# Float16 pairs for the gate and up products of FFN groups two and three, in a hybrid attention and mLSTM diffusion layer

## The chip, the cores and the metric

The kernel runs on one core of a Trainium2 chip. The metric is the device time of one execution in microseconds (us), the median of three runs. One more execution is taken by the profiler; its busy times, waits and clocks are those quoted here. The engines are called PE (TensorE; its weight loads, which run beside its matmuls, are PEld), DVE (VectorE), ACT (ScalarE), POOL (GpSimd) and SP (SyncE, which issues nearly all transfers).

## What is computed

The reference is one step of a diffusion backbone with one layer. There are 128 context tokens and 1024 latent tokens, 1152 in all; the model width is 1024 and the FFN width 2816. All arithmetic is float32. Cut to what matters here:

```python
def trunk_layer(x, mods, ...):
    sh1, sc1, g1, sh2, sc2, g2 = mods          # from silu(cond) @ w_ada + b_ada
    h = rmsnorm(x, norm1_w) * (1 + sc1) + sh1
    ... = split(h @ w_in, ...)                 # attention q, k, v; mLSTM q, k, v, o, gates
    attn_o = attention(aq, keys, vals)         # 8 query heads of 64, 2 kv heads, rope
    hm, st_f, st_b = mlstm_bidir(...)          # 4 heads of 128, forward and backward
    x = x + g1 * (concatenate([attn_o, hm]) @ w_out)
    h2 = rmsnorm(x, norm2_w) * (1 + sc2) + sh2
    x = x + g2 * swiglu(h2, w_gu, w_down)
    return x, ...

def swiglu(h, w_gu, w_down):
    g, u = split(h @ w_gu, 2, axis=-1)
    return (silu(g) * u) @ w_down
```

The outputs are the final RMS norm of x for both kinds of token, new keys and values of the context, and the mLSTM states.

## The kernel before

**Stages.** The 1152 tokens are nine blocks of 128, and three blocks make a chunk of 384 tokens. The kernel goes through: load, first norm and modulation (about 0 to 60 us); keys, values, gates and the attention's query projection (60 to 165); four mLSTM heads, with the attention of chunk 0 woven between (165 to 520); the prefill, which is the output projection and second norm of chunk 0 (520 to 617); then the FFN of chunks 0, 1 and 2 (617 to 938, 938 to 1284, 1284 to 1572), the attention of the next chunk being woven beside the first two. The change calls the FFN of these three chunks groups one, two and three.

**Products of nearly float32 precision.** A float32 operand is split into a high part and a rest (hi and lo), and a product is three matmuls: hi·hi, hi·lo, lo·hi. In the FFN both parts are of type fp32r, of four bytes. In the projections of the first stages they are float16 pairs, which needs the operands scaled by a power of two so that they lie in float16's range: class `Scaled` takes the largest absolute value of a weight, by ACT passes with an accumulated sum (an upper bound of the maximum), and `power_scale` (L166–177) turns a bound per partition into a power of two on all partitions. `power_scale` is a small chain over engines: PE transposes the column (L116), DVE reduces it to one number (L171) and makes a power of two and its inverse from its bits in four steps (`powers`, L161–164), PE broadcasts them by a matmul with a row of ones (L175, operands `pv` and `one`), and DVE copies the result (L176).

**An FFN chunk.** `gate_up` (L1319–1341) goes through 22 tiles f of 128 FFN columns, in groups of 4 or 5. For each f it loads a gate piece and an up piece of w_gu (128 partitions x 1024, 512 KB) with `load_piece` (L140–154): SP's transfer into `raw` (two buffers), ACT's cast to the high part `whi` (L152, five buffers), DVE's subtraction for the low part `wlo` (L137, five buffers). Then `products` (L1313–1317) runs 24 matmuls of 128x384 for the piece: eight k, three products each, on the features h2 of the chunk (`aTh`, `aTl`: transposed, 8 x 128 x 384). The activation is tanh on ACT (L1333), two products on DVE (L1334, L1335), a cast on ACT (L1338) and a subtraction on POOL. `down` (L1343–1355) multiplies by w_down in the same fp32r form, 128x512, from pieces loaded in the same way.

**The features.** `norm2` (L1282–1311) makes h2 of a block: ACT scales the row by its inverse norm (`y`, L1294), PE transposes (L116), DVE applies scale2 and shift2 (`fl`, L1304; for chunk 0 also ACT, L1302), ACT casts to `aTh` (L1309), and DVE (POOL in chunk 0) subtracts for `aTl`. norm2 of the next chunk is woven into the `down` of the last group of f (12 to 16 and 17 to 21 are the last two groups; L1479–1481). scale2 and shift2 are computed long before, by the generator `ada`, which finishes just ahead of `kwork` near the end of the query projection (L979–980).

**What sets the order.** Every engine runs its own queue in order. `weave` and `emit` set in which order instructions are written out; a planner with its own costs and priorities (`hot(n)`) then fixes the order on every engine from that. A tile that is reallocated under the same tag waits for the last user of its buffer. Around 162 to 172 us, PE runs four transposes of `qr` (the attention's queries) and then the 72 query matmuls of the first mLSTM head (`q_group`, L808–810); DVE runs the steps of a small inverse square root (L131–133), the copy of `QT` (L654), a 128x1024 subtraction for a float16 pair (`ipair`, L137), subtractions for `qT` and rotary products (L679).

Of the kernel before, what the change touches and what calls it, by code (L numbers as in the profile page):

```python
# [8 lines left out]
F32 = mybir.dt.float32  # L9
F32R = mybir.dt.float32r  # L10
F16 = mybir.dt.float16
BF16 = mybir.dt.bfloat16
# [7 lines left out]
P = 128  # L20
# [25 lines left out]
def hybrid_step(ctx: ExitStack, tc: tile.TileContext, I: dict, O: dict):  # L46
# [11 lines left out]
    def nm(s):  # L58
        uid[0] += 1
        return f"{s}_{uid[0]}"  # L60
# [10 lines left out]
    def emit(gen):  # L71
        for _ in gen:
            pass
# [62 lines left out]
    def sub(out, full, hi, eng):  # L136
        (dve if eng == "dve" else pool).tensor_tensor(out=out, in0=full, in1=hi, op=ALU.subtract)  # L137

    def load_piece(srcs, shape, raw=None, own=None):

        a, b = shape
        n = a * b

        def view(t):
            return t[:, :n].rearrange("p (a b) -> p a b", b=b)

        raw = raw or wp.tile([P, 1024], F32, name=nm("raw"), tag="raw", bufs=2)
        hi = own[0] if own else wp.tile([P, 1024], F32R, name=nm("whi"), tag="whi", bufs=5)
        lo = own[1] if own else wp.tile([P, 1024], F32R, name=nm("wlo"), tag="wlo", bufs=5)
        for part, ap_ in srcs:  # L150
            dma(part(view(raw)), ap_)
        nc.scalar.copy(hi[:, :n], raw[:, :n])  # L152
        sub(lo[:, :n], raw[:, :n], hi[:, :n].bitcast(F32), "dve")
        return view(hi), view(lo)
# [78 lines left out]
    bcol = cp.tile([P, 48], F32, name="bcol")  # L233
    ncol = cp.tile([P, 16], F32, name="ncol")
    vsc = cp.tile([P, 4], F32, name="vsc")

    es_a = ExitStack()
    pA = es_a.enter_context(tc.tile_pool(name="pA", bufs=4, space=PSUM, reuse_waits="tile"))
# [738 lines left out]
    emit(steps)  # L977
    groups_in[1].made = groups_in[1].pairs()
    emit(ada)  # L979
    emit(kwork)  # L980
    es_r.close()
    es_h.close()
# [94 lines left out]
    def a_tiles():  # L1077
        return (hp.tile([P, KD, CT], F32R, name=nm("aTh"), tag="b2"),
                hp.tile([P, KD, CT], F32R, name=nm("aTl"), tag="b3"))

    def new_x1(c):
        x1 = hp.tile([P, CB, D], F32, name=nm("x1"), tag=f"b{4 + c % 2}")
# [199 lines left out]
    def norm2(c, a, i):  # L1282

        x1 = a["x1"][i]
        if "h2" not in a:
            a["h2"] = a_tiles()
        th, tl = a["h2"]
        r = a["rs"][i]
        both = ap2.tile([P, KD, P], F32, name=nm("fl"), tag="pr", bufs=2)
        cnd = 0 if c * CB + i == 0 else 1  # L1290
        for half in range(2):
            with hot(800):
                y = fp.tile([P, 512], F32, name=nm("y"), tag="y", bufs=2)
                act(y, x1[:, half * 512 : (half + 1) * 512], AF.Copy, scale=r)  # L1294
                ps = bank()
                for j in range(4):
                    transpose(ps[:, j * P : (j + 1) * P], y[:, j * P : (j + 1) * P])
                full = both[:, half * 4 : half * 4 + 4]
                for j in range(4):
                    k = half * 4 + j  # L1300
                    if j == 0 and c == 0:
                        act(full[:, j, :], ps[:, j * P : (j + 1) * P], AF.Identity, scale=scale2[:, k, cnd : cnd + 1], bias=shift2[:, k, cnd : cnd + 1])  # L1302
                        continue
                    dve.tensor_scalar(  # L1304
                        out=full[:, j, :], in0=ps[:, j * P : (j + 1) * P],
                        scalar1=scale2[:, k, cnd : cnd + 1], scalar2=shift2[:, k, cnd : cnd + 1],
                        op0=ALU.mult, op1=ALU.add)
                oh = th[:, half * 4 : half * 4 + 4, i * P : (i + 1) * P]
                nc.scalar.copy(oh, full)  # L1309
                sub(tl[:, half * 4 : half * 4 + 4, i * P : (i + 1) * P], full, oh.bitcast(F32), "pool" if c == 0 else "dve")  # L1310
            yield True

    def products(ps, wh, wl, th, tl):  # L1313
# [2 lines left out]
            mm(ps, wh[:, k, :], tl[:, k, :], start=False, stop=False)  # L1316
            mm(ps, wl[:, k, :], th[:, k, :], start=False, stop=(k == KD - 1))  # L1317

    def gate_up(a, f0, nf):  # L1319
        th, tl = a["h2"]  # L1320
        acts = a["act"] = []
        for f in range(f0, f0 + nf):
            if True:
                pg, pu = bank(), bank()
                for off, ps in ((0, pg), (D_FF, pu)):
                    src = w_gu[:, off + f * P : off + (f + 1) * P].rearrange("(k p) n -> p k n", p=P)
                    wh, wl = load_piece([(full_view, src)], (KD, P))
                    products(ps[:, 0:CT], wh, wl, th, tl)
                    yield 6
                parts = [(slice(0, CT), pg[:, 0:CT], pu[:, 0:CT])]  # L1330
            tn = fp.tile([P, CT], F32, name=nm("tn"), tag="tn", bufs=2)
            for cs, g, u in parts:
                act(tn[:, cs], g, AF.Tanh, scale=0.5)  # L1333
                dve.scalar_tensor_tensor(out=tn[:, cs], in0=tn[:, cs], scalar=1.0, in1=u, op0=ALU.add, op1=ALU.mult)  # L1334
                dve.tensor_tensor(out=tn[:, cs], in0=tn[:, cs], in1=g, op=ALU.mult)  # L1335
# [98 lines left out]
    for tag, bufs in (("gl", 1), ("gx", 1), ("t2", 3)):  # L1434
        ft.tile([P, 512], F32, name=f"lay_{tag}", tag=tag, bufs=bufs)
    fp = ctx.enter_context(tc.tile_pool(name="fp", bufs=1, side="right", reuse_waits="tile"))

    cur, nxt = {}, {}
    cur["x1"], nxt["x1"] = new_x1(0), new_x1(1)
# [11 lines left out]

    def groups(c, a, lst):
        for f0, nf in lst:
            yield from gate_up(a, f0, nf)
            yield from down(c, a, f0, nf, 0)
            yield from down(c, a, f0, nf, 1)

# [10 lines left out]
    for c in range(NCH):  # L1468
        if c + 1 < NCH:
            main = groups(c, cur, GROUPS[:NG])  # L1470
            for _ in range(4):
                next(main)
            weave(main, chain(previous(c, cur), att), 18 * sum(nf for _, nf in GROUPS[:NG]) - 24, 50)
            emit(att)
            attn_out(nxt, oT, out_gates())
            emit(groups(c, cur, GROUPS[NG:-1]))
            f0, nf = GROUPS[-1]
            emit(gate_up(cur, f0, nf))
            n2 = chain(*[norm2(c + 1, nxt, i) for i in range(CB)])  # L1479
            weave(chain(down(c, cur, f0, nf, 0), down(c, cur, f0, nf, 1)), n2, 6 * nf, 8)  # L1480
            emit(n2)
            if c + 2 < NCH:
                oT = []
                att = attention(c + 2, oT, set())
            nxt["prev"] = cur
            cur = nxt
            nxt = cur["next"] = {}
        else:
            main = groups(c, cur, LAST[:-1])
            for _ in range(4):  # L1490
                next(main)
            weave(main, previous(c, cur), 24, 3)
            emit(main)
            emit(gate_up(cur, *LAST[-1]))
            down_last(c, cur, *LAST[-1])


# [50 lines left out]
```

## Time and profile before

| | |
|---|---|
| median of 3 runs | 1574.08 us (1573.49 to 1574.66) |
| the profiled execution's own time | 1574.08 us |
| its span, first to last instruction | 1572.3 us |
| mean granted clock of PE | 0.979 |
| read from and written to memory | 183.79 MB, 13.26 MB |
| gate/up matmuls 128x384 fp32r (L1315–1317) | 3 x 1056, 353 to 356 us busy each |
| float16 matmuls 128x384 of a head's projection (L484) | 288, 94.1 us busy |
| casts and subtractions of weight pieces | 216 each, 222.3 us of ACT, 260.4 us of DVE (some of another shape among them) |

How to read it: a row of a group has the line, the engine, the operation, the output and its inputs, the shape, the count, then busy time and the mean of one in ns, then the idle time of the engine just before them and what ended it. A timeline row has start and duration in us first, and idle time with its releaser in brackets. Matmuls are pipelined, so a duration overlaps the next start; the rate of a stream is read from its starts. A window's row has the busy time and count of each engine, the granted clock of PE, the mean busy share of the 16 DMA engines, and GB/s.

### The profile page before, as it was taken

What the parts mean: (1) busy time and instruction counts of PE and PEld (TensorE: products, weight loads), DVE (VectorE), ACT (ScalarE), POOL (GpSimd) and SP (SyncE); (2) the same over time, 40 slices, a digit from 0 to 9 for tenths busy, and PEclk for the clock granted to TensorE, in tenths of its full rate; (3) what the DMA queues carried; (4) which work ended last, traced back from release to release, by engine and by line L of the source; (5) the groups of instructions that cost most, each with busy time, mean ns of one, the idle gap of its engine ahead of it and who ended that gap; (6) DMA issues with size and microseconds to landing.
All of it is one profiled execution on the core that took longest, in us unless ns stands there. A gap on an engine that the chain in (4) does not pass through costs nothing.

```text
span 1572.3 us, 23397 instructions
## 1 busy us (share of the span) xinstructions
PE 1487.7 (95%) x8539; PEld 1247.3 (79%) x8539; DVE 1022.9 (65%) x2025; ACT 771.8 (49%) x1409; POOL 271.4 (17%) x357
## 2 busy tenths in 40 slices
PE   6899999999999689999999999999999999999996
PEld 3544567676766468898998989989898989999995
DVE  4878554737659576677555677877866585554555
ACT  4754465847656344545432444556552443323332
POOL 0213333322343242100110101000010101001111
PEclk9899999999999799999999999999999999999998
DMA  9664323523556847767555447878763545544441
GB/s 360 186 182 157 97 68 41 121 47 68 114 150 162 265 80 197 184 174 175 154 154 149 147 126 236 195 170 180 179 162 114 168 133 168 161 130 138 143 139 54
DMA packets 387881, 236.91 MB, mean 151 GB/s; under 512 B 170198, under 2 KB 346790, under 8 KB 387766
## 3 DMA queue, kind: packets, MB, share of 16 engines
q1 hardware_dynamic: 385110, 231.84, 54.1%
q10 hardware_dynamic: 2656, 3.58, 1.1%
q8 instruction: 67, 1.10, 0.3%
q14 instruction: 48, 0.39, 0.1%
HBM read 183.79 MB, written 13.26 MB: 125 GB/s over the span
## 4 chain that ended last, share of the span: by engine, by line
PE 77%; DVE 11%; DMA 5%; ACT 4%; issue 2%; SPq 0%; POOL 0%; ACTq 0%; DVEq 0%; POOLq 0%
PE mm L1316 11%; PE mm L1317 11%; PE mm L1315 11%; PE mm L1115 5%; PE mm L1116 5%; PE mm L1117 5%; PE S L1035 3%; PE wi L483 3%; PE wi L485 3%; PE wi L484 3%; PE mm L116 2%; PE mm L1147 1%; PE mm L1148 1%; PE mm L1149 1%; PE po L1060 1%
## 5 line engine op out<-in xcount | busy, mean ns | idle before, releaser
L152 ACT CAST whi<-raw 128x1024 fp32r<-128x1024 f32 (+1 forms) x216 | 222.3, 1029 | 411.0 <-PE mm L1316 156.5
L137 DVE TENSOR_TENSOR wlo<-raw,whi 128x1024 fp32r<-128x1024 f32 (+1 forms) x216 | 260.4, 1206 | 202.9 <-ACT whi L152 202.3
L1316 PE MATMUL mm<-aTl,whi 128*128 128x384 f32 x1056 | 355.7, 337 | 2.7 <-DVE aTl L137 2.7
L1317 PE MATMUL mm<-aTh,wlo 128*128 128x384 f32 x1056 | 354.3, 336 | 0.0
L1315 PE MATMUL mm<-aTh,whi 128*128 128x384 f32 x1056 | 353.3, 336 | 0.0
L137 POOL TENSOR_TENSOR hl<-tn,hl 128x384 fp32r<-128x384 f32 x66 | 84.4, 1279 | 840.0 <-ACT hl L1338 748.3
L1316 PEld LDWEIGHTS mm<-aTl,whi 128*128 128x128 f32 x1056 | 198.5, 188 | 3.9 <-DVE aTl L137 3.3
L1315 PEld LDWEIGHTS mm<-aTh,whi 128*128 128x128 f32 x1056 | 198.1, 188 | 0.6
L1317 PEld LDWEIGHTS mm<-aTh,wlo 128*128 128x128 f32 x1056 | 198.4, 188 | 0.0
L1116 PE MATMUL mm<-wlo,hl 128*128 128x512 f32 x372 | 145.7, 392 | 0.0
L1115 PE MATMUL mm<-whi,hl 128*128 128x512 f32 x372 | 144.3, 392 | 0.0
L1117 PE MATMUL mm<-whi,hl 128*128 128x512 f32 x372 | 143.4, 392 | 0.0
L483 PE MATMUL wi<-ipair,hT 128*128 128x384 f16 (+2 forms) x408 | 135.6, 335 | 1.7 <-ACT hT L507 1.2
L484 PE MATMUL wi<-ipair,hT 128*128 128x384 f16 (+2 forms) x408 | 135.6, 335 | 0.0
L485 PE MATMUL wi<-ipair,hT 128*128 128x384 f16 (+2 forms) x408 | 132.1, 335 | 1.0 <-DVE hT L137 1.0
L1042 DVE SCALAR_TENSOR_TENSOR pl<-pr,st,ph 128x1152 f16<-128x1152 f32 (+1 forms) x72 | 96.0, 1333 | 31.7 <-ACT ph L1041 31.4
L1037 DVE TENSOR_REDUCE st<-S 128x1 f32<-128x1152 f32 (+1 forms) x72 | 88.9, 1235 | 16.3 <-PE S L1035 16.1
L1038 ACT ACTIVATE pr<-S,st 128x1152 f32<-128x1152 f32 (+1 forms) x72 | 81.3, 1130 | 32.4 <-DVE st L1037 29.3
L1041 ACT ACTIVATE ph<-pr,st 128x1152 f16<-128x1152 f32 (+1 forms) x72 | 83.9, 1165 | 23.8 <-DVE st L1040 6.7
L1035 PE MATMUL S<-kst,qT 128*128 128x384 f32 (+1 forms) x400 | 87.6, 349 | 4.8 <-ACT pr L1038 4.8
L1104 DVE TENSOR_TENSOR t<-mm,gl 128x512 f32<-128x512 f32 x102 | 69.1, 687 | 26.2 <-DMA gl<-g_d 11.5
L1117 PEld LDWEIGHTS mm<-whi,hl 128*128 128x128 f32 x372 | 69.9, 188 | 14.2
(375 smaller groups left out, 2538.4 us busy)
## 6 DMA issues: line engine op xcount, KB each, us to landing
raw<-in_w_gu_dram SPq DMA_DIRECT2D x132, 512.0 KB
raw<-in_w_down_dram SPq DMA_DIRECT2D x60, 512.0 KB
a<-in_w_ada_dram SPq DMA_DIRECT2D x24, 512.0 KB
gl<-g_d SPq DMA_DIRECT2D x36, 256.0 KB
aw<-in_w_ada_dram SPq DMA_DIRECT2D x16, 512.0 KB
iraw<-in_w_in_dram SPq DMA_DIRECT2D x32, 256.0 KB
raw<-in_w_out_dram SPq DMA_DIRECT2D x12, 512.0 KB
x<-in_x_sample_dram SPq DMA_DIRECT2D x11, 512.0 KB
```

Source lines behind the costliest of these rows:

```text
L137: (dve if eng == "dve" else pool).tensor_tensor(out=out, in0=full, in1=hi, op=ALU.subtract)
L152: nc.scalar.copy(hi[:, :n], raw[:, :n])
L483: mm(ps[:, :n], ah, wh[:, k % 2, c0 : c0 + n], start=(k == 0), stop=False)
L484: mm(ps[:, :n], ah, wl[:, k % 2, c0 : c0 + n], start=False, stop=False)
L485: mm(ps[:, :n], al, wh[:, k % 2, c0 : c0 + n], start=False, stop=(k == KD - 1))
L1035: mm(S[:, n, 0:w], qT[:, h, :], kst[kv][:, t, c0 + n * w : c0 + (n + 1) * w], start=(t == 0), stop=(t == 1))
L1115: mm(ps, ah, wh[:, k % 2, :], start=(k == 0), stop=False)
L1116: mm(ps, ah, wl[:, k % 2, :], start=False, stop=False)
L1117: mm(ps, al, wh[:, k % 2, :], start=False, stop=(k == nk - 1))
L1315: mm(ps, wh[:, k, :], th[:, k, :], start=(k == 0), stop=False)
L1316: mm(ps, wh[:, k, :], tl[:, k, :], start=False, stop=False)
L1317: mm(ps, wl[:, k, :], th[:, k, :], start=False, stop=(k == KD - 1))
```

## The change

Five things are changed; the lines are those of the kernel before.

1. For chunks 1 and 2, gate and up use float16 pairs. `gate_piece` takes the place of `load_piece` there: ACT makes hi as a scaled copy, DVE makes lo in one multiply-and-subtract, both in one buffer of 4 KB per partition, from the tag of `whi` for gate and of `wlo` for up. h2 of these chunks is a float16 pair in one buffer of its own: `half_tiles` gives chunk 1 one of the two buffers of `aTh` and `aTl`, and chunk 2 the other.
2. Chunk 0 keeps fp32r, and an added ACT pass for each of its 44 gate and up pieces (Abs of the 128x1024 raw piece, output to a scratch tile in bfloat16) accumulates sums into `gsum`.
3. `bound_h2` is written out between `ada` and `kwork`: the largest |shift2| and |scale2| bound h2 (norm rows are at most the square root of D), `power_scale` makes the power of two, and scale2 and shift2 are multiplied by it in place; tiny steps keep the inverses.
4. `bound_w_gu` is written out after the last `gate_up` of chunk 0: it reduces `gsum`, runs `power_scale` for the weights' scale, and sets the inverses for chunks 1 and 2.
5. The tanh takes its scale, and the second product its factor, from these inverses in every chunk, so that the second product becomes a fused form. The tiles `guc`, `gsum`, `one2` and two unused ones (`lay_cp`, `lay_fp`) bring the pools to multiples of 128 bytes per partition.

PE has 8130 matmul instructions where it had 8126, DVE 24 instructions more, ACT 44 more; POOL has as many as before.

```diff
+    guc = cp.tile([P, 8], F32, name="guc")
+    gsum = cp.tile([P, 2 * NF], F32, name="gsum")
+    one2 = cp.tile([1, P], F32, name="one2")
+    dve.memset(one2, 1.0)
+    cp.tile([P, 8], F32, name="lay_cp")
...
     emit(ada)
+    def inverses_gu(inv):
+        dve.tensor_scalar(out=guc[:, 4:5], in0=inv, scalar1=0.5, scalar2=None, op0=ALU.mult)
+        dve.tensor_tensor(out=guc[:, 5:6], in0=inv, in1=inv, op=ALU.mult)
+    def bound_h2():
+        b2 = gp.tile([P, 2], F32, name="b2")
+        dve.tensor_reduce(out=b2[:, 0:1], in_=shift2, axis=AX.XY, op=ALU.max, apply_absolute_value=True)
+        dve.tensor_reduce(out=b2[:, 1:2], in_=scale2, axis=AX.XY, op=ALU.max, apply_absolute_value=True)
+        dve.scalar_tensor_tensor(out=b2[:, 1:2], in0=b2[:, 1:2], scalar=float(D) ** 0.5, in1=b2[:, 0:1], op0=ALU.mult, op1=ALU.add)
+        emit(power_scale(gp, one1, b2[:, 1:2], guc[:, 0:2]))
+        for t in (scale2, shift2):
+            dve.tensor_scalar(out=t, in0=t, scalar1=guc[:, 0:1], scalar2=None, op0=ALU.mult)
+        inverses_gu(guc[:, 1:2])
+    def bound_w_gu():
+        b2 = fp.tile([P, 2], F32, name="b2w", tag="s1", bufs=3)
+        dve.tensor_reduce(out=b2[:, 0:1], in_=gsum, axis=AX.X, op=ALU.max)
+        emit(power_scale(fp, one2, b2[:, 0:1], guc[:, 2:4]))
+        dve.tensor_tensor(out=guc[:, 6:7], in0=guc[:, 1:2], in1=guc[:, 3:4], op=ALU.mult)
+        inverses_gu(guc[:, 6:7])
+    bound_h2()
     emit(kwork)
...
+    def half_tiles(c):
+        t = hp.tile([P, 2, KD, CT], F16, name=nm("hF"), tag=("b2", "b3")[c % 2])
+        return t[:, 0], t[:, 1]
...
-            a["h2"] = a_tiles()
+            a["h2"] = a_tiles() if c == 0 else half_tiles(c)
...
+    def gate_piece(a, c, i, src):
+        if c == 0:
+            raw = wp.tile([P, 1024], F32, name=nm("raw"), tag="raw", bufs=2)
+            jk = fp.tile([P, 1024], BF16, name="jg") if "jg" not in a else a["jg"]
+            a["jg"] = jk
+            pieces = load_piece([(full_view, src)], (KD, P), raw=raw)
+            act(jk, raw, AF.Abs, accum_out=gsum[:, i : i + 1])
+            return pieces
+        raw = wp.tile([P, 1024], F32, name=nm("raw"), tag="raw", bufs=2)
+        w = wp.tile([P, 2, 1024], F16, name=nm("wf"), tag=("whi", "wlo")[i % 2], bufs=5)
+        dma(raw.rearrange("p (k n) -> p k n", k=KD), src)
+        hi, lo = w[:, 0], w[:, 1]
+        act(hi, raw, AF.Copy, scale=guc[:, 2:3])
+        dve.scalar_tensor_tensor(out=lo, in0=raw, scalar=guc[:, 2:3], in1=hi, op0=ALU.mult, op1=ALU.subtract)
+        return tuple(v.rearrange("p (k n) -> p k n", k=KD) for v in (hi, lo))
...
-                    wh, wl = load_piece([(full_view, src)], (KD, P))
+                    wh, wl = gate_piece(a, c, 2 * f + (off > 0), src)
...
-                act(tn[:, cs], g, AF.Tanh, scale=0.5)
+                act(tn[:, cs], g, AF.Tanh, scale=guc[:, 4:5])
                 dve.scalar_tensor_tensor(out=tn[:, cs], in0=tn[:, cs], scalar=1.0, in1=u, op0=ALU.add, op1=ALU.mult)
-                dve.tensor_tensor(out=tn[:, cs], in0=tn[:, cs], in1=g, op=ALU.mult)
+                dve.scalar_tensor_tensor(out=tn[:, cs], in0=tn[:, cs], scalar=guc[:, 5:6], in1=g, op0=ALU.mult, op1=ALU.mult)
...
+    fp.tile([P, 16], F32, name="lay_fp")
...
             emit(gate_up(c, cur, f0, nf))
+            if c == 0:
+                bound_w_gu()
```

More of the change, by code (lines that the diff above doesn't have):

```diff
@@ L1309, in norm2 @@
                 nc.scalar.copy(oh, full)
-                sub(tl[:, half * 4 : half * 4 + 4, i * P : (i + 1) * P], full, oh.bitcast(F32), "pool" if c == 0 else "dve")
+                sub(tl[:, half * 4 : half * 4 + 4, i * P : (i + 1) * P], full, oh.bitcast(F32) if c == 0 else oh, "pool" if c == 0 else "dve")
             yield True
@@ L1317, in products, with gate_up @@
             mm(ps, wl[:, k, :], th[:, k, :], start=False, stop=(k == KD - 1))
-    def gate_up(a, f0, nf):
+    def gate_piece(a, c, i, src):
[13 more added lines that the diff above has]
+        return tuple(v.rearrange("p (k n) -> p k n", k=KD) for v in (hi, lo))
+    def gate_up(c, a, f0, nf):
         th, tl = a["h2"]
@@ L1453, in groups @@
         for f0, nf in lst:
-            yield from gate_up(a, f0, nf)
+            yield from gate_up(c, a, f0, nf)
             yield from down(c, a, f0, nf, 0)
@@ L1477, in hybrid_step @@
             f0, nf = GROUPS[-1]
-            emit(gate_up(cur, f0, nf))
+            emit(gate_up(c, cur, f0, nf))
+            if c == 0:
+                bound_w_gu()
             n2 = chain(*[norm2(c + 1, nxt, i) for i in range(CB)])
@@ L1493, in hybrid_step @@
             emit(main)
-            emit(gate_up(cur, *LAST[-1]))
+            emit(gate_up(c, cur, *LAST[-1]))
             down_last(c, cur, *LAST[-1])
```

## The prediction

> **What bounds the kernel now.** I read the page's head first (busy shares, and the chain of work that ended last).
>
> ```profile
> span 1572.3 us, 23397 instructions
> ...
> PE 1487.7 (95%) x8539; PEld 1247.3 (79%) x8539; DVE 1022.9 (65%) x2025; ACT 771.8 (49%) x1409; POOL 271.4 (17%) x357
> ...
> PE 77%; DVE 11%; DMA 5%; ACT 4%; issue 2%; SPq 0%; POOL 0%; ACTq 0%; DVEq 0%; POOLq 0%
> ```
>
> TensorE (PE) is busy 95% of the span, and 77% of the chain is its own work. So two things move the time: shorter matmuls where PE never waits, and new waits in front of PE. A mean over the span does not say where it never waits; the busy time of each engine in chosen stretches does (us; busy us and count of PE, weight loads, DVE, ACT, POOL; granted clock; DMA share; GB/s):
>
> ```profile
> 165.00:410.00 245.00, 239.24 (x1532) 169.25 (x1532) 145.47 (x386) 153.86 (x425) 79.58 (x168) 0.98 0.34 74
> 520.00:617.00 97.00, 77.64 (x382) 62.06 (x383) 63.98 (x122) 44.44 (x66) 30.94 (x24) 0.93 0.61 163
> 660.00:760.00 100.00, 100.00 (x558) 90.96 (x557) 72.61 (x100) 50.17 (x65) 8.11 (x6) 1.00 0.73 177
> 1000.00:1100.00 100.00, 100.00 (x594) 93.44 (x594) 79.39 (x111) 59.75 (x81) 6.79 (x7) 1.00 0.81 178
> 1290.00:1400.00 110.00, 110.00 (x594) 104.64 (x593) 58.34 (x83) 38.37 (x52) 13.12 (x10) 1.00 0.50 152
> ```
>
> In the FFN stretches (660–760 is chunk 0, 1000–1100 chunk 1, 1290–1400 chunk 2) PE is busy all the time at full clock, and DVE and ACT have room. What a matmul loses there, the kernel loses. The head stage (165–410) is nearly as full (239 of 245 us): a new wait there is not absorbed later. Only the prefill (520–617) has idle PE time.
>
> **The gain: gate and up of chunks 1 and 2.** Per chunk these are 22 f × 2 pieces × 24 matmuls = 1056 of 128x384, so 2112 change from fp32r to float16. The kernel already has float16 matmuls of that shape, in its query and head projections. First the groups by shape (mean ns after the busy time), then single starts from the timeline of PE.
>
> ```profile
> L1316 PE MATMUL mm<-aTl,whi 128*128 128x384 f32 x1056 | 355.7, 337 | 2.7 <-DVE aTl L137 2.7
> ...
> L484 PE MATMUL wi<-ipair,hT 128*128 128x384 f16 x288 | 94.1, 327 | 0.0
> ```
>
> ```profile
> 173.05 0.33 PE L810 MATMUL wi<-hT,ipair 128*128 128x384 f16 x1
> ...
> 185.08 0.33 PE L484 MATMUL wi<-ipair,hT 128*128 128x384 f16 x1
> ...
> 1300.09 0.33 PE L1316 MATMUL mm<-aTl,whi 128*128 128x384 f32 x1
> ...
> 1320.37 0.33 PE L1316 MATMUL mm<-aTl,whi 128*128 128x384 f32 x1
> ```
>
> The durations overlap, so the distance between starts counts. The float16 pair of rows lies 74 starts apart: 12.03 us / 74 = 162.5 ns. The fp32r pair lies 117 starts apart: 20.28 / 117 = 173.3 ns. The gain is 10.8 ns × 2112 = **22.9 us**; the means of the groups (337 and 327) would give 10 × 2112 = 21 us.
>
> Would DVE or ACT take it back? Per piece, the cast (L152) and subtraction (L137) become a scaled float16 copy and a fused multiply-subtract; rows of these forms exist:
>
> ```profile
> L137 DVE TENSOR_TENSOR wlo<-raw,whi 128x1024 fp32r<-128x1024 f32 x204 | 252.1, 1236 | 184.4 <-ACT whi L152 183.7
> L152 ACT CAST whi<-raw 128x1024 fp32r<-128x1024 f32 x204 | 214.8, 1053 | 379.3 <-PE mm L1316 143.6 <-DMA raw<-in_w_gu_dram 110.2 <-PE mm L1117 88.4
> ...
> L219 DVE SCALAR_TENSOR_TENSOR ipair<-iraw,isc,ipair 128x1024 f16<-128x1024 f32 x10 | 13.1, 1307 | 5.5 <-ACT ipair L218 5.5
> L218 ACT ACTIVATE ipair<-iraw,isc 128x1024 f16<-128x1024 f32 x10 | 11.6, 1156 | 5.5 <-PE wi L485 5.4
> ...
> L1335 DVE TENSOR_TENSOR tn<-tn,mm 128x384 f32<-128x384 f32 x66 | 36.5, 552 | 1.6
> L1334 DVE SCALAR_TENSOR_TENSOR tn<-tn,mm 128x384 f32<-128x384 f32 x66 | 36.4, 552 | 64.4 <-PE mm L1317 64.1
> ```
>
> ACT +103 ns and DVE +71 ns on each of 88 pieces (9.1 and 6.2 us in all), beside PE in stretches where DVE idles 20 of 100 us and ACT 40. The tn product that becomes a fused one costs nothing (552 ns both). I cost these at 0; without the cover it is the DVE rival below. The raw buffer is freed about 0.17 us later per piece, small against a 4.16 us piece (24 × 173.3).
>
> **bound_h2, ahead of the first mLSTM head.** In the built order PE now runs the four transposes of qr, the transpose of the bound, the power-of-two broadcast (`pv,one`) and two score matmuls, and only then the 72 query matmuls of the first mLSTM head (q_group, L808–810), which earlier stood directly behind the qr transposes. DVE computes the power between those two, in its own order: a reduce, then a 2.69 us subtraction, a qT subtraction and four rotary products lie between the first and last step of the small chain. These are the rows in the timelines of PE and DVE, and the PE clock (column PEclk) of two windows:
>
> ```profile
> 162.43 0.60 PE L116 MATMUL mm<-ident,qr 128*128 128x128 f32 x4
> 165.01 0.32 PE L808 MATMUL wi<-hT,ipair 128*128 128x384 f16 x1 [1.98 <-DVE QT L654]
> ```
>
> ```profile
> 165.67 2.69 DVE L137 TENSOR_TENSOR ipair<-iraw,ipair 128x1024 f16<-128x1024 f32 x1 [0.42 <-ACT ipair L222]
> 168.39 0.68 DVE L137 TENSOR_TENSOR qT<-mm,qT 64x512 fp32r<-64x512 f32 x1
> 169.11 1.43 DVE L679 TENSOR_TENSOR nr<-qraw,ss 128x256 f32<-128x256 f32 x4
> ```
>
> ```profile
> 162.00:166.00 4.00, 2.02 (x15) 0.98 0.42 121
> 166.00:169.00 3.00, 3.00 (x11) 0.50 0.34 102
> ```
>
> The rotary products end at 170.5; with the last two steps, the small matmul and its hand-over, PE resumes near 171.5–172.5 instead of 165.0: 6.5 to 7.5 us of wait. The first of the two score matmuls may fall inside it, and the wait of 1.98 us with the half-clock stretch behind it (11 starts in 3 us where 18 would fit, about 1.1 us) merges with the new one. Everything queued behind on PE (this head and all later ones) waits too. Bounds: 2 us if the scheduler's order holds but the large subtraction comes earlier than in the old trace, 9 if a half-clock stretch follows that is twice as long. I take **+6**.
>
> **44 Abs passes in chunk 0.** Each is an ACT pass over 128x1024 with an accumulator read; the nearest rows:
>
> ```profile
> L1278 ACT ACTIVATE jk<-x 128x1024 bf16<-128x1024 f32 x15 | 15.8, 1056 | 2.9 <-DVE x L1105 1.8 <-POOL x L1105 1.1
> L1038 ACT ACTIVATION_READ_ACCUMULATOR pr<-S,st 128x1 f32 x72 | 14.2, 198 | 0.0
> ```
>
> That is 1.25 us each, 55 us of ACT in all. In the built order nearly every one stands directly behind its cast, beside the DVE subtraction of the same buffer (1.24 us, above), so the raw buffer comes free at about the same moment; in 660–760 ACT was busy only 50 of 100 us, with the cover gone at worst 1.25 us a piece. I take **+1** for chunk 0 (0 to 5). Three of them run in the prefill, where PE does wait for ACT:
>
> ```profile
> 542.24 1.06 ACT L152 CAST whi<-raw 128x1024 fp32r<-128x1024 f32 x1 [1.86 <-DMA raw<-in_w_gu_dram]
> 544.64 1.34 ACT L1294 ACTIVATE y<-x,ry 128x512 f32<-128x512 f32 x2 [1.35 <-DVE ry L133]
> ...
> 548.48 0.65 ACT L1309 CAST aTh<-fl 128x512 fp32r<-128x512 f32 x1
> ```
>
> The first fits the 1.35 us of idle time before y; the second and third stand between y and aTh, on the chain to chunk 0's first operand. At 1.25 us each that is 0 to 3.75; I take **+1.5**.
>
> **bound_w_gu, between gate/up and down of chunk 0's last group.** PE's order becomes: last gate/up matmul, transpose of the bound, `pv,one`, then the down matmuls. Nothing of PE lies between the two, while DVE does tn (0.55), reduce, the second tn (0.55), one step, a wlo subtraction (1.24) and three steps. A bare chain of the same kind, from transpose to broadcast, without strangers between:
>
> ```profile
> 42.71 0.27 PE L116 MATMUL mm<-ident,hbd 128*1 128x128 f32 x1 [0.86 <-DVE hbd L399]
> 43.94 0.58 PE L175 MATMUL mm<-pv,one 1*128 1x2 f32 x2 [0.96 <-DVE pv L164]
> ```
>
> 1.23 + 0.55 + 1.24, plus hand-overs: 3.1–3.3 us idle where the timeline had none:
>
> ```profile
> 915.00 0.33 PE L1317 MATMUL mm<-aTh,wlo 128*128 128x384 f32 x1
> 915.40 0.60 PE L116 MATMUL mm<-ident,y 128*128 128x128 f32 x4
> ...
> 939.95 0.44 PE L1316 MATMUL mm<-aTl,whi 128*128 128x384 f32 x1 [1.03 <-DVE aTl L137]
> ...
> 1286.10 0.44 PE L1316 MATMUL mm<-aTl,whi 128*128 128x384 f32 x1 [1.64 <-DVE aTl L137]
> ```
>
> Then a half-clock stretch as at 166–169, 1.1 to 1.7 us. The Trainium skill ("TensorE: Matmul & The Clock Gate", section "HAM oscillation — how this bites in real kernels") describes the same re-throttle and re-warm cost after micro-idles; the 0.50 of 166–169 agrees. Sum **+4.5** (2 to 6; 2 where the transpose waits less because DVE takes the chain first, and the 1.03 us wait at 939.95 goes). Chunk 1 to 2 keeps its 1.64 us wait; h2 of chunk 2 now has a slot of its own and needn't wait for the old one: 0 (−2 to 0). The pool paddings and the few small DVE steps in guc: 0; they move addresses, and the trace has nothing that depends on one.
>
> **Sum.** −22.9 + 6 + 1 + 1.5 + 4.5 = **−9.9 us**. The profiled execution's own time is 1574.08 (span 1572.3 and 1.8 around it), which equals the median of the three runs. Forecast **1564.2**. All lower bounds: −22.9 + 2 + 0 + 0 + 2 − 2 = −20.9, 1553.2. All upper ones: −22.9 + 9 + 5 + 3.75 + 6 = +0.85, 1574.9.
>
> **The rivals.**
> - *The waits are mostly absorbed* (bound_h2 2, chunk 0 0.5, prefill 1, bound_w_gu 2: +5.5): 1574.1 − 17.4 = **1556.7**. For it: the built order is no timetable, and DVE may reach the small steps earlier. Against: in the old trace DVE has the large subtraction exactly there.
> - *DVE becomes the bound beside the attention of chunk 1.* 79.4 of 100 us busy; at the faster pace (100 us of work in about 95) and with 71 ns more on some 20 pieces it is (79.4 + 1.4)/95 = 85%. If half of chunk 1's 11.4 us gain is lost to waits on wlo: 1564.2 + 5.7 = **1569.9**. For it: the share. Against: of L1316's waits above, 2.7 us in 1056 matmuls, all are on aTl and none on a weight.
> - *Slower: ACT on the reload of raw in chunk 0.* Two raw buffers; one is reused after its cast, its subtraction and now its Abs. If the planner's casts of other pieces go ahead of the Abs, the reload starts 1.25 us later. A piece has 4.16 us of PE time. With 20 of the 44 pieces late by all of it, a number I choose as nearly half: 25 us in place of the 1, **1588.2**. It turns the sum to slower from (9.9 + 1 + 3.1) / 44 = 0.32 us a piece. For it: DMA share 0.73 in 660–760. Against: ACT half idle, Abs directly behind the cast.
> - *It does not do what it says: the matmul takes as long in float16 there.* Operands from other slots and a weight load per matmul could set the same 173 ns; nothing gained, the costs stay: 1574.1 + 13 = **1587**. Against: 162.5 ns in the same kernel with the same number of weight loads. The Trainium skill ("TensorE: Matmul & The Clock Gate", section "Back-to-back issue gap") gives a gap from columns and clock alone, N / 2.4 + 2.5 ns, which is 162.5 for 384 columns whatever the type, and by that nothing would be gained by the type; the trace disagrees for fp32r (173.3).
>
> **How the numbers follow.** Chances: forecast 0.50; absorbed waits 0.21; DVE bound 0.15; all costs at their upper bounds (1574.9) 0.05; ACT on the reload 0.07; no gain per matmul 0.02. Range 1553.2 to 1574.9, the bounds of the sum; it leaves out the two slower cases (0.09) and some misses. A measurement of this kernel tells about 0.2%, 3.1 us, from no change: faster is below 1570.9, slower above 1577.2. Faster: 0.50 + 0.21 and about half of the DVE case, 0.08: 0.79. Same: the rest of it and the upper bounds, 0.12. Slower: 0.09.
>
> **What would show it.** Starts of gate/up in chunks 1 and 2 lie 162 ns apart; chunk 2 shrinks by some 11 us. PE waits 6 to 7 us around 165–172 on DVE's pv. A 3 us gap behind chunk 0's last gate/up, with PEclk down behind it. ACT Abs rows of 1.25 us and no new PE waits on whi or raw in 617–915. I am wrong if PE waits for wlo in 1000–1100, or if the Abs passes delay raw.

## The result and the profile after

The changed kernel takes 1592.15 us (median of 4 runs, 1588.05 to 1595.3) where the kernel before took 1573.78 in the same sessions: a ratio of 1.012, 95% interval 1.0103 to 1.0137. It is 18 us slower; the forecast was 10 us faster. Its profiled execution took 1591.97 us. The head of its page, and then the busy times of the same kinds of stretch as before (chunk 0, 1 and 2 begin 15, 26 and 25 us later):

```profile
span 1590.2 us, 23410 instructions
...
PE 1482.1 (93%) x8545; PEld 1093.6 (69%) x8545; DVE 1033.3 (65%) x2049; ACT 828.2 (52%) x1497; POOL 262.8 (17%) x357
```

```profile
660.00:760.00 100.00, 97.06 (x531) 86.53 (x530) 70.19 (x97) 61.27 (x86) 7.24 (x6) 1.00 0.70 169
1000.00:1100.00 100.00, 95.47 (x546) 69.75 (x545) 82.34 (x111) 58.13 (x72) 5.69 (x5) 1.00 0.75 178
1310.00:1420.00 110.00, 108.09 (x602) 70.42 (x602) 61.73 (x88) 41.57 (x55) 10.67 (x10) 0.98 0.49 156
```

PE was busy for all of these stretches before; now it is idle for 2 to 5 us in each. The float16 matmuls are as fast as forecast. These two rows of PE's timeline, in chunk 2, are 97 starts apart: 15.76 us / 97 = 162.5 ns.

```profile
1385.10 0.33 PE L1351 MATMUL mm<-hF,wf 128*128 128x384 f16 x1
...
1400.86 0.33 PE L1352 MATMUL mm<-hF,wf 128*128 128x384 f16 x1
```

**Where the time went.** I cut each profile at the starts of matmuls that all kernels have: the 121st of before's L483 (late in the query projection), the 25th of L808 (the second mLSTM head), the 24th of L1147 (output projection), the first of gate and up of chunk 0, its last, the first of chunk 1, the first of chunk 2, and the end of the last matmul. Stage lengths in us, from one profile each (the experiments are told below):

| stage | before | changed | e2 | e5 | e6 | e7 | e8 | e4 | e9 | e10 | e12 |
|---|---|---|---|---|---|---|---|---|---|---|---|
| to the query projection | 140.9 | 142.2 | 140.2 | 143.5 | 141.8 | 142.5 | 139.8 | 140.9 | 141.2 | 141.5 | 141.6 |
| bound_h2, first head | 79.2 | 86.7 | 86.3 | 78.0 | 86.5 | 86.9 | 78.0 | 77.8 | 77.5 | 77.7 | 78.1 |
| other heads | 284.4 | 284.4 | 281.3 | 282.3 | 285.8 | 285.8 | 282.3 | 282.9 | 281.4 | 281.4 | 285.1 |
| prefill | 110.5 | 116.7 | 117.5 | 116.7 | 115.9 | 110.0 | 110.2 | 110.9 | 110.1 | 109.9 | 110.9 |
| chunk 0 | 299.9 | 305.0 | 299.1 | 305.1 | 304.0 | 303.0 | 301.0 | 300.0 | 299.0 | 299.6 | 301.1 |
| chunk 0's last down | 23.5 | 29.0 | 28.7 | 28.6 | 25.9 | 28.6 | 25.2 | 23.9 | 24.2 | 23.5 | 24.7 |
| chunk 1 | 345.5 | 344.4 | 343.8 | 345.3 | 343.3 | 344.8 | 344.2 | 341.6 | 342.6 | 346.2 | 342.7 |
| chunk 2 | 275.3 | 268.9 | 265.8 | 265.6 | 266.4 | 266.0 | 266.0 | 268.2 | 266.1 | 265.2 | 266.0 |

Changed against before: 1.3 + 7.5 + 0 + 6.2 + 5.1 + 5.5 − 1.1 − 6.4 = +18.1 us. The stage of the other heads, where these kernels hardly differ, varies by 4.5 us from profile to profile, so differences of a few us in a single stage need a second witness.

**bound_h2.** The timelines of PE and DVE of the changed kernel show the forecast wait:

```profile
165.89 0.27 PE L116 MATMUL mm<-ident,b 128*1 128x128 f32 x1 [1.55 <-DVE rt L132]
171.70 0.55 PE L175 MATMUL mm<-pv,one 1*128 1x2 f32 x2 [5.54 <-DVE pv L164]
172.62 0.66 PE L1066 MATMUL S<-kst,qT 128*128 128x128 f32 x2 [0.36 <-DVE guc L176]
173.08 0.54 PE L813 MATMUL wi<-hT,ipair 128*128 128x384 f16 x1
```

```profile
166.19 0.28 DVE L171 TENSOR_REDUCE pv<-mm 1x1 f32<-1x128 f32 x1 [0.16 <-PE mm L116]
166.40 2.75 DVE L137 TENSOR_TENSOR ipair<-iraw,ipair 128x1024 f16<-128x1024 f32 x1
...
170.02 1.41 DVE L684 TENSOR_TENSOR nr<-qraw,ss 128x256 f32<-128x256 f32 x4
...
171.42 0.13 DVE L164 TENSOR_SCALAR pv<-pv 1x1 f32<-1x1 f32 x1
```

Between the reduce at 166.19 and the last step at 171.42 lie a 2.75 us subtraction and the rotary products, as read from the built order; the head's first matmul starts at 173.08 where it started at 165.01. Behind it PE's clock is at half, and 12 matmuls start in 3 us (11 in the 3 us of before's 166 to 169); here the starts are 0.32 us apart until 177.6:

```profile
173.00:176.00 3.00, 3.00 (x12) 1.49 (x12) 2.62 (x7) 0.85 (x3) 0.93 (x1) 0.50 0.00 0
```

**bound_w_gu.** In the changed kernel's PE timeline the broadcast waits 2.81 us, and the window behind it (PEclk is the seventh value behind the stretch, 0.58) is at a low clock:

```profile
935.34 0.27 PE L116 MATMUL mm<-ident,b2w 128*1 128x128 f32 x1
938.42 0.38 PE L175 MATMUL mm<-pv,one 1*128 1x2 f32 x2 [2.81 <-DVE pv L164]
```

```profile
939.00:943.00 4.00, 4.00 (x14) 3.23 (x14) 2.42 (x9) 1.34 (x2) 0.00 (x0) 0.58 0.44 131
```

**Prefill.** The timeline of ACT: of three Abs passes (L1361), one stands ahead of `y` (L1329) and two between `y` and `aTh` (L1344), the chain to the first block of chunk 0's features.

```profile
551.76 1.05 ACT L1361 ACTIVATE jg<-raw 128x1024 bf16<-128x1024 f32 x1
...
553.56 1.34 ACT L1329 ACTIVATE y<-x,ry 128x512 f32<-128x512 f32 x2 [0.66 <-DVE ry L133]
554.80 1.04 ACT L1361 ACTIVATE jg<-raw 128x1024 bf16<-128x1024 f32 x1
...
559.23 1.06 ACT L1361 ACTIVATE jg<-raw 128x1024 bf16<-128x1024 f32 x1
...
560.29 0.61 ACT L1344 CAST aTh<-fl 128x512 fp32r<-128x512 f32 x1
```

The first gate matmul comes only at 630, and PE has no wait for `aTh` itself. What grows are its waits for `mx`, the operand of the output projection. Two rows of PE's waits before (504 to 617) and two of the changed kernel (513 to 632), each with the us in all, the number of waits and the longest:

```profile
PE mm L1147 <- ACT mx L1184: 2.9, 3, 1.6
PE mm L1149 <- DVE mx L137: 1.1, 1, 1.1
```

```profile
PE mm L1182 <- ACT mx L1219: 5.9, 5, 2.3
PE mm L1184 <- DVE mx L137: 3.7, 2, 2.6
```

That is 9.6 us against 4.0. Other waits shrink by some 2 us, and PE's mean clock is 0.90 against 0.92. In e7, told below, which takes these three passes out of the prefill, the two rows are at 2.9 and 1.1 us again.

**Chunk 1.** The windows of the whole chunk, before and changed, and PE's longest waits in the changed one:

```profile
938.30:1283.90 345.60, 344.57 (x1924) 317.63 (x1922) 255.71 (x378) 176.65 (x234) 26.07 (x22) 1.00 0.66 169
```

```profile
964.00:1308.40 344.40, 335.88 (x1923) 238.53 (x1921) 254.08 (x376) 180.54 (x231) 25.92 (x22) 1.00 0.66 169
```

```profile
PE po L1090 <- DMA phT<-ph: 2.8, 1, 2.8
PE mm L1350 <- DVE tn L1386: 1.9, 1, 1.9
PE po L1091 <- DMA plT<-pl: 1.6, 3, 0.6
PE mm L1150 <- DVE t L1139: 0.9, 1, 0.9
```

PE is busy 8.7 us less, and idle 8.5 us where it was idle 1.0. About half of the waits are for transfers of the attention (`phT`, `plT`), nearly all others for steps of DVE. None is for a weight piece (`wf`), and DVE is busy no longer than before (254.1 us, 255.7).

**What I had not looked for: the down matmuls.** They are fp32r in both kernels, with the same shapes. Two rows of a stream in chunk 2 of the kernel before (35 starts apart) and two of the changed kernel (43 starts apart):

```profile
1339.76 0.39 PE L1115 MATMUL mm<-whi,hl 128*128 128x512 f32 x1
...
1347.69 0.39 PE L1117 MATMUL mm<-whi,hl 128*128 128x512 f32 x1
```

```profile
1412.47 0.39 PE L1151 MATMUL mm<-wlo,hl 128*128 128x512 f32 x1
...
1422.50 0.40 PE L1152 MATMUL mm<-whi,hl 128*128 128x512 f32 x1
```

7.93 / 35 = 226.6 ns before, 10.03 / 43 = 233.3 after. Over all starts of down matmuls that follow each other by less than 245 ns, the means are 227.8 and 232.5. There are 3 x 372 + 72 = 1188 such matmuls, so this is 6 to 8 us. In the built programs, `hl` (the activations, the stationary operand here) begins at byte 116224 of a partition before and at 114048 after. The first is a multiple of 512, the second lies 128 past a multiple of 256: pool fp grew by the Abs scratch tile (2048 bytes), `lay_fp` (64) and small tiles (64).

### The profile page after: what moved, and what is told of

It reads as the page before. It is cut to its first block, busy times and chain, and to the rows that moved or that the text cites. A ratio compares the mean times of both kernels' runs of the same rounds, so it can differ in the third digit from the quotient of the medians.

```text
span 1590.2 us, 23410 instructions
## 1 busy us (share of the span) xinstructions
PE 1482.1 (93%) x8545; PEld 1093.6 (69%) x8545; DVE 1033.3 (65%) x2049; ACT 828.2 (52%) x1497; POOL 262.8 (17%) x357
## 5 line engine op out<-in xcount | busy, mean ns | idle before, releaser
L137 DVE TENSOR_TENSOR wlo<-raw,whi 128x1024 fp32r<-128x1024 f32 (+1 forms) x128 | 152.6, 1194 | 132.5 <-ACT whi L152 132.1
L1351 PE MATMUL mm<-hF,wf 128*128 128x384 f16 x704 | 230.3, 327 | 3.0 <-DVE hF L137 3.0
L1350 PE MATMUL mm<-hF,wf 128*128 128x384 f16 x704 | 229.0, 327 | 2.7 <-DVE tn L1386 2.7
L1352 PE MATMUL mm<-hF,wf 128*128 128x384 f16 x704 | 230.1, 327 | 0.0
L137 POOL TENSOR_TENSOR hl<-tn,hl 128x384 fp32r<-128x384 f32 x66 | 77.3, 1172 | 850.1 <-ACT hl L1390 775.1
L152 ACT CAST whi<-raw 128x1024 fp32r<-128x1024 f32 (+1 forms) x128 | 128.5, 1005 | 144.5 <-DMA raw<-in_w_down_dram 48.0
L1367 ACT ACTIVATE wf<-raw,guc 128x1024 f16<-128x1024 f32 x88 | 100.6, 1148 | 145.4 <-DMA raw<-in_w_gu_dram 127.4
L1368 DVE SCALAR_TENSOR_TENSOR wf<-raw,guc,wf 128x1024 f16<-128x1024 f32 x88 | 113.1, 1286 | 62.2 <-ACT wf L1367 61.6
L1351 PE MATMUL mm<-aTl,whi 128*128 128x384 f32 x352 | 118.6, 337 | 0.0
L1352 PE MATMUL mm<-aTh,wlo 128*128 128x384 f32 x352 | 118.5, 337 | 0.0
L1350 PE MATMUL mm<-aTh,whi 128*128 128x384 f32 x352 | 118.2, 336 | 0.0
L1352 PEld LDWEIGHTS <-wf 128*128 128x128 f16 x704 | 69.0, 98 | 48.4 <-issue 4.5
L1351 PEld LDWEIGHTS <-wf 128*128 128x128 f16 x704 | 69.1, 98 | 47.8 <-issue 4.6
```

Source lines behind the costliest of these rows:

```text
L1350: mm(ps, wh[:, k, :], th[:, k, :], start=(k == 0), stop=False)
L1368: dve.scalar_tensor_tensor(out=lo, in0=raw, scalar=guc[:, 2:3], in1=hi, op0=ALU.mult, op1=ALU.subtract)
```

## The experiments

The theory after the result had four parts: the two bounds stall PE, the Abs passes stall the prefill, the address of `hl` slows the down matmuls, and chunk 1 gets nothing from its faster matmuls. The rival to each is that the time belongs to something else and only moves. Ratios are to the kernel before on the same chip, with 95% intervals.

**e1 and e2: the address of hl.**

```diff
-    fp.tile([P, 16], F32, name="lay_fp")
+    fp.tile([P, 112], F32, name="lay_fp")      # e1; e2: [P, 48]
```

> The changed kernel with 384 bytes more of padding in pool fp, so that the activations hl (the stationary operand of the down matmuls) start at a multiple of 512 bytes, as they did before the change; in the changed kernel they start at 128 bytes past a multiple of 256. Theory (the address of hl slows the down matmuls): their starts return from about 232 ns to 226.5 ns apart, and the time falls by 5 to 10 us, to 1582 to 1587. Rival (the slower starts come from other traffic or the clock): 232 ns stays and the time stays within 2 us of 1592.

> The changed kernel with 128 bytes more of padding in pool fp: hl starts at a multiple of 256 bytes, but not of 512. If 256 bytes are what matters, as in the run with 512 (226.5 ns, 1582 to 1587); if 512 matter, as the changed kernel (232 ns, 1592).

Measured: e1 1584.83 us, 1.0092 (1.0071 to 1.0112); e2 1581.42 us, 1.0065 (1.0043 to 1.0088). The order on every engine is that of the changed kernel, and the padding moves `hl`, and `gx` and `mx`, which have its place earlier, and no other tile. The timeline of e1 (45 starts apart):

```profile
1409.72 0.39 PE L1152 MATMUL mm<-whi,hl 128*128 128x512 f32 x1
...
1419.92 0.39 PE L1151 MATMUL mm<-wlo,hl 128*128 128x512 f32 x1
```

10.20 / 45 = 226.7 ns, and the median distance in e2 is 227 as well: a multiple of 256 is enough. Chunk 2 falls from 268.9 to 266.0 and 265.8 us. By the ratios e1 is 4 us under the changed kernel, less than expected, and e2 9 us, though both have the same order and the same spacing: one total alone is not to be read more closely than that.

**e3: the same address in the kernel before, nothing else.**

```diff
+    fp.tile([P, 32], F32, name="lay_fp")
```

> The kernel before with 128 bytes of padding in pool fp and nothing else: hl starts at 128 bytes past a multiple of 256. Theory (address): down starts go from 226.5 to about 232 ns, time 1574 plus 6 to 10, so 1580 to 1584. Rival (not the address): 1574, 226.5 ns.

Measured: 1574.79 us, 1.0027 (1.0013 to 1.0041). Two rows of its timeline, 29 starts apart:

```profile
1336.72 0.40 PE L1117 MATMUL mm<-whi,hl 128*128 128x512 f32 x1
...
1343.23 0.40 PE L1115 MATMUL mm<-whi,hl 128*128 128x512 f32 x1
1343.47 0.40 PE L1116 MATMUL mm<-wlo,hl 128*128 128x512 f32 x1
```

6.75 / 29 = 232.8 ns. The spacing is what was expected, in the kernel before and without any other edit; the order on every engine is that of the kernel before. The time moved by 4 us (2 to 6.5), less than the 6 to 10 that were expected. The padding moves `mx` as well, the stationary operand of the output projection; those matmuls start 230 ns apart before and 233 ns here on the mean.

**e4 and e9: the float16 form without its costs.** Constant scales, neither bound, no Abs; e4 keeps hl where the changed kernel has it, e9 has it at a multiple of 256.

```diff
+    dve.memset(guc, 1.0)
+    dve.memset(guc[:, 4:5], 0.5)
-    bound_h2()
-            if c == 0:
-                bound_w_gu()
-            act(jk, raw, AF.Abs, accum_out=gsum[:, i : i + 1])
-    fp.tile([P, 16], F32, name="lay_fp")
+    fp.tile([P, 32], F32, name="lay_fp")      # e4; e9: [P, 64]
```

> The changed kernel without both bounds and without the 44 Abs passes: the scales are constants written at the start (1 for both operands), the float16 form of chunks 1 and 2 and all addresses stay. It leaves out the computation of the scales. Theory (bounds and Abs cost about 7.7 us ahead of the heads, 6 in the prefill, 3 in chunk 0 and 5 behind it, and the float16 form gains some 11 us less than 22.9 because of the down matmuls): 1592 less 20, 1568 to 1574. Rival (the bounds are cheap, chunks 1 and 2 lose by themselves): 1580 or more.

> As e4_const (constant scales, no bounds, no Abs; it leaves out the computation of the scales), with hl at a multiple of 256 bytes. It is what the float16 form is worth without its costs. Theory (5.5 ns on some 1180 down matmuls): 5 to 7 us under e4_const, ratio to the kernel before about 0.992; chunk 2 takes 266 us instead of 268. If e8_all_three has hidden nearly all costs, it is within 5 us of this one. Rival (the address counts less than by the spacing): ratio 0.995 or more.

Measured: e4 1564.42 us, 0.996 (0.9945 to 0.9975); e9 1558.98 us, 0.9922 (0.9902 to 0.9942). So bounds and Abs cost 1.012 − 0.996 = 1.6%, 25 us, and all of the float16 form without them and with a good address is worth 12 us, not 22.9. e4 and e9 differ in the padding alone, with the same order on every engine: 0.4%, 6 us, is a second witness for the price of the address.

**e5, e6, e7, e8: each cost taken away by place, then all.** All have hl at a multiple of 256. e5 runs bound_h2 inside the first head; e6 puts down matmuls between the transpose and the broadcast of bound_w_gu; e7 reads the high parts of the first three pieces for their Abs beside pieces 3 to 5; e8 does all three.

```diff
-        emit(power_scale(gp, one1, b2[:, 1:2], guc[:, 0:2]))
+        yield from power_scale(gp, one1, b2[:, 1:2], guc[:, 0:2])
-    bound_h2()
-    weave(head_project(0, sts[0]), beside((att, 0.1),), 96, 96)
+    bnd = bound_h2()
+    weave(head_project(0, sts[0]), beside((att, 0.1), (bnd, 0.06)), 96, 96)
+    emit(bnd)
...
-                bound_w_gu()
+            bnd = bound_w_gu() if c == 0 else iter(())
+            next(bnd, None)
+            weave(and_then(chain(down(...), down(...)), bnd, 1), n2, 6 * nf, 8)
...
+            if i < 3:
+                wait.append((i, jk.rearrange("p (k n) -> p k n", k=KD), pieces[0].bitcast(F32)))
+                todo = []
+            elif wait:
+                todo.append(wait.pop(0))
```

> As e2_hl256, with one part changed: the bound of the features is run inside the first mLSTM head, its transpose and its broadcast many matmuls apart. Theory (PE's wait of 5.5 us between the two, with the half clock behind it, costs 8 to 9 us): 8 us under e2_hl256, that is a ratio to the kernel before of about 1.001. Rival (the wait only moves: the heads wait elsewhere for the same DVE work): less than 3 us under e2_hl256, ratio 1.005 to 1.0065.

> As e2_hl256, with one part changed: the broadcast of the weights' bound is written out behind the second part of the down product, so that down matmuls stand between its transpose and its broadcast. Theory (3 us of PE wait and the slow clock behind it): 4 to 5 us under e2_hl256, ratio about 1.0035. Rival (the scale then comes late for the first float16 pieces of chunk 1, and PE waits there): no gain, and the first float16 matmuls wait on wf.

> As e2_hl256, with one part changed: the Abs passes of the first three gate and up pieces read the high part later, beside pieces 3 to 5, so that none runs in the prefill. Theory (three passes of 1.25 us on ACT's chain from y to aTh, and the order that follows from them, cost the 6 to 7 us by which the prefill is longer): 5 to 7 us under e2_hl256, ratio about 1.0025, prefill 110 to 112 us from the first output projection to the first gate matmul. Rival (other causes in the prefill, such as the order of the attention of chunk 1): prefill stays at 117.

> All three of e5, e6 and e7 together, with hl at a multiple of 256 bytes. If the costs add: 10 - 8 - 4 - 6 = 8 us under the kernel before, ratio about 0.995, faster than both kernels. Rival (they share a cause, or chunk 0's other 41 Abs passes cost as much): ratio 0.998 to 1.002.

Measured: e5 1577.78 us, 1.0042 (1.0027 to 1.0056); e6 1584.09, 1.0081 (1.0064 to 1.0098); e7 1581.52, 1.0057 (1.0037 to 1.0076); e8 1563.62, 0.9954 (0.994 to 0.9969). In the stage that each one touches, the table shows the saving: e5 takes 8.3 us off the first head (86.3 to 78.0), e6 2.8 us off chunk 0's last down, e7 7.5 us off the prefill. The totals missed what was expected of them: against e2's ratio e5 falls by 4 us (8 expected), e7 by 1 (5 to 7), and e6 rises by 3 (4 to 5 less expected). In the profiles of e6 and e7 the other heads take 4.5 us longer than in e2, where these edits touch nothing, and chunk 0 takes 4 to 6 us longer in all three; e7 moves its three passes into chunk 0, the other two change nothing there. Why these stages differ stays open. With all three the total is 0.995, as expected of the sum, and e8 is faster than both kernels. In e8's timeline of PE, fourteen down matmuls stand where PE waited:

```profile
911.71 0.27 PE L116 MATMUL mm<-ident,b2w 128*1 128x128 f32 x1
911.73 0.48 PE L1155 MATMUL mm<-whi,hl 128*128 128x512 f32 x1
...
915.13 0.38 PE L175 MATMUL mm<-pv,one 1*128 1x2 f32 x2
```

**e12: the other Abs passes.** e8 with all Abs left out, the sums set to a constant.

> As e8_all_three without any Abs pass: the sums that bound the weights are a constant, so the bound leaves out its data; the small chains stay. Theory (the remaining 41 to 44 passes beside DVE's subtraction cost chunk 0 about 1 us): chunk 0 takes 300 us, time within 2 us of e8_all_three. Rival (they delay the reload of raw or ACT's other work): 3 to 6 us less than e8_all_three, ratio 0.992 to 0.9935.

Measured: 1564.17 us, 0.9953 (0.9934 to 0.9971), chunk 0 301.1 us. The Abs passes, all 44 of which e8 runs in chunk 0, cost nothing there that can be seen.

**e10: float16 in chunk 2 alone.** From e8; chunk 1 uses `load_piece` and `a_tiles`, and bound_w_gu follows chunk 1.

```diff
+        if c == 1:
+            return load_piece([(full_view, src)], (KD, P))
-            bnd = bound_w_gu() if c == 0 else iter(())
+            bnd = bound_w_gu() if c == 1 else iter(())
```

> As e8_all_three, but chunk 1 keeps fp32r and only chunk 2 has the float16 pairs; the weights' bound moves behind chunk 1's last gate and up. Theory (in chunk 1 the float16 matmuls gain 11 us and lose nearly all of it to new waits at its start and on the attention of chunk 2): the time is within 3 us of e8_all_three, chunk 1 takes 345 us. Rival (chunk 1's gain is real, and the stage tables only mix it with other effects): 8 to 11 us slower than e8_all_three, ratio about 1.001.

Measured: 1563.34 us, 0.9952 (0.9934 to 0.9971), the same as e8. Chunk 1's conversion is worth nothing here that can be seen; the two intervals leave room for some 4 us. Chunk 1 takes 346.2 us against 344.2, but here it also holds the weights' bound, which e8 has in chunk 0's last down (25.2 against 23.5).

**e11: the attention in chunk 1 without priority.**

```diff
-                att = attention(c + 2, oT, set())
+                att = attention(c + 2, oT, set(), 0, 0)
```

> As e8_all_three, with the attention that is woven into chunk 1 given no priority in the planner (0 where 200 stood). Theory (PE's new waits in chunk 1 come from attention matmuls that stand too early in PE's order for the softmax and transfers ahead of them): the waits on phT, plT and pr in 990 to 1020 go, 3 to 5 us less, ratio about 0.993. Rival (they come from DVE falling behind with the weight pieces and tn): no change, ratio 0.995 to 0.996.

Measured: 1562.36 us, 0.9949 (0.993 to 0.9967), chunk 1 344.9 us. No change: PE is idle for 10.2 us of chunk 1, 9.4 in e8, and still waits for the attention (`pr`, `phT`), at other places.

**e13 and e14: chunk 1 without the attention.** e8 and e10 with `att = iter(())` in chunk 1.

> As e8_all_three, without the attention of chunk 2 that is woven into chunk 1's FFN (it leaves that attention out; the output projection of chunk 2 reads the attention of chunk 1 instead). Chunk 1 then holds the FFN, the output projection and norm alone. Theory (the attention's chains are what eats chunk 1's gain): chunk 1 is 9 to 11.4 us shorter here than in e14, the same kernel with fp32r in chunk 1. Rival (the start and the end of the chunk and DVE's weight pieces eat it): at most 5 us shorter.

> As e10_only_chunk2 (fp32r in chunk 1), without the attention of chunk 2 in chunk 1, as in e13. Its chunk 1 is what e13's is held against: about 1056 x 10.8 ns = 11.4 us longer by the theory, 5 us or less by the rival.

Measured: e13 1508.42 us, 0.96 (0.9582 to 0.9618); e14 1513.79 us, 0.9629 (0.9598 to 0.9659). Chunk 1 takes 290.6 and 295.3 us: 4.7 us of the 11.4 remain, so the rival holds for more than half. PE is idle for 6.5 us of chunk 1 in e13 and for 1.4 in e14, which is 5 of the 6.7 us lost. Two of these waits are seen in the timelines of e13, of DVE and then of PE:

```profile
954.26 4.07 DVE L1430 SCALAR_TENSOR_TENSOR x<-x,ry,fw 128x512 f32<-128x512 f32 x6
958.24 1.28 DVE L1381 SCALAR_TENSOR_TENSOR wf<-raw,guc,wf 128x1024 f16<-128x1024 f32 x1
959.43 0.55 DVE L1399 SCALAR_TENSOR_TENSOR tn<-tn,mm 128x384 f32<-128x384 f32 x1
...
988.82 1.28 DVE L1381 SCALAR_TENSOR_TENSOR wf<-raw,guc,wf 128x1024 f16<-128x1024 f32 x1 [2.32 <-ACT wf L1380]
990.03 1.88 DVE L1138 TENSOR_TENSOR t<-mm,gl 128x512 f32<-128x512 f32 x3
```

```profile
958.56 0.33 PE L1357 MATMUL mm<-hF,wf 128*128 128x384 f16 x1
960.04 0.32 PE L1355 MATMUL mm<-hF,wf 128*128 128x384 f16 x1 [1.15 <-DVE tn L1399]
...
987.81 0.39 PE L1157 MATMUL mm<-whi,hl 128*128 128x512 f32 x1
990.77 0.79 PE L1155 MATMUL mm<-whi,hl 128*128 128x512 f32 x1 [2.57 <-DVE t L1138]
991.36 0.63 PE L1156 MATMUL mm<-wlo,hl 128*128 128x512 f32 x1
```

At 988.82 DVE stands 2.32 us before a weight piece that ACT has not yet made, and the step that empties a PSUM bank of `down` (L1138; PE writes its sums to these banks) is queued behind it; PE waits 2.57 us for that bank, and its next matmul comes 0.59 us behind the first where 0.227 is usual. At 954.26 the six final products of chunk 0 (4.07 us) and a weight piece stand ahead of `tn`, for which PE waits 1.15 us. These two are waits by the order in DVE's queue; DVE is busy for 172 of the 291 us of this chunk.

## Why the prediction was wrong, point by point

- **Gain per matmul: right.** 162.5 ns against 173.3.
- **"What a matmul loses there, the kernel loses", and "I cost these at 0" for the cover of the weight pieces: wrong, the largest miss.** The forecast took 11.4 us in each chunk. Chunk 1 gave 1.1 and chunk 2 6.4 (9.3 with hl in place). In chunk 1 PE has 7.5 us of new waits, and its down matmuls are slower by some 2 us (396 of them). e10 shows that chunk 1's conversion moves the time by nothing that can be seen, and e13 against e14 that more than half of its gain goes without any attention beside it. I read free time from a window (79 of 100 us busy); in the timelines shown, what counts is which instruction stands ahead of the one that frees PE's next bank or operand. The DVE rival named the place and priced it at 5.7 us, half of what it was. Its mechanism is not what the timelines show: it expected waits on `wlo`, and PE waits for no weight piece in chunk 1; DVE is busy 82 of 100 us. So the sign "if PE waits for wlo in 1000–1100" did not come, and the forecast failed there all the same. Whether the steps come late because of the 71 and 103 ns added to a piece or because PE now arrives earlier, no run separates. e11 removes none of it, so the share that the attention adds is not settled further.
- **"The pool paddings ... 0; they move addresses, and the trace has nothing that depends on one": wrong.** The address of `hl` is worth 5 to 7 ns on each of 1188 matmuls: e3 makes the kernel before slower by it, and the spacing is undone in e1 and e2. It is 6 to 8 us by the spacing, 6 by e4 and e9, 4 by e3's time.
- **Prefill: the cause right, the size wrong, and the path only in part right.** 1.5 us was taken, with 3.75 as the end; the stage grew by 6.2, and e7 and e8, without the three passes, bring it back to 110. The passes do stand on ACT's chain to `aTh`, 3.75 us for all three, but what grew are PE's waits for `mx`, by 5.6 us, as attention and output projection change places behind the late `aTh`. That last part was read from the timelines, not tried by itself.
- **bound_h2: right.** +6 (2 to 9) forecast; the stage grew by 7.5, and e5 takes 8.3 off.
- **bound_w_gu: right.** +4.5 (2 to 6) forecast; the stage grew by 5.5. e6 and e8 take about 3 off. The Trainium skill ("TensorE: Matmul & The Clock Gate", section "HAM oscillation — how this bites in real kernels"), which the prediction names for the slow clock behind the wait, speaks of idle gaps above some 3.4 us, and it is the section behind that one that speaks of micro-idles; here a wait of 2.81 us was followed by a clock of 0.58.
- **Abs beside chunk 0: right.** +1 forecast, e12 against e8 shows 0. The slower rival, ACT on the reload of raw, did not happen. The 5.1 us by which the changed kernel's chunk 0 is longer are 1.4 to 2 us of slower down matmuls (306 x 4.7 to 6.7 ns) and 2.7 us more of idle PE (4.9 against 2.2). The stage takes 299 to 305 us over these kernels, and the cause of that spread stays open.
- The changed kernel is slower for none of the reasons that the rival on the slower side named: it is the sum of a gain that came to a third, and of costs that were 24 us instead of 13.

## What to carry to other kernels

A faster matmul is worth its time only if what frees its operands and banks keeps up at every hand-over: read each engine's queue at the hand-overs of a stage, not its busy share over the stage. A small chain over two engines (PE transposes, DVE reduces, PE broadcasts) cost 5.5 and 7.5 us here with its two PE steps side by side in the order; with 14 matmuls between them it cost about 2 us (e8's last down of chunk 0), and with 79 nothing that can be seen (e5, e8). After any edit to a pool, compare the starts of streams that the edit does not touch, and the addresses of their operands.

## What the runs showed of the hardware that was not expected

Matmuls of 128x512 in fp32r start 226.6 to 226.7 ns apart when their stationary operand begins at a multiple of 256 or of 512 bytes of a partition, and 232.8 to 233.3 ns apart when it begins 128 bytes past a multiple of 256, in two kernels and with the same order of instructions. The Trainium skill ("SBUF — State Buffer", section "Operand start alignment") asks only that an operand start at a multiple of its element size, and names no cost; by these runs that is not enough for the full rate. Gate and up in fp32r kept 173 ns though their tiles moved by 768 bytes, three times 256. Other distances from a multiple of 256 were not tried.
